# Two chained transformer blocks on one core: a modelled clock for TensorE's order, and block 2 attention on row halves

## The chip, the core and the metric

The kernel runs on one NeuronCore of a Trainium2 chip. The metric is the device time of one execution, in microseconds. The core's engines run each their own queue of instructions: TensorE (PE, with its weight loads as PEld), VectorE (DVE), ScalarE (ACT), GpSimd (POOL) and SyncE (SP, which here issues most DMAs).

## What is computed

Block 1 takes x (512 tokens, 1024 wide): a mixer with one input projection and four groups of heads (dilated attention, stick-breaking attention, a sliding window with sinks, block-sparse attention), cross attention into 256 memory tokens, and an MLP with squared ReLU. Its output is x of block 2, which has two layers. Each layer works on the 512 tokens ("latent") and, in layer 0 fully, on 256 context tokens. The parts that the change touches:

```python
for l in range(DEPTH_2):                                  # 2
    mod_lat = (silu_c @ ada_w[l] + ada_b[l])[:, None, :]  # modulation: 1024 -> 6*1024
    mod_ctx = silu_cc @ ada_w[l] + ada_b[l]
    ...
    q_lat = apply_rope(qk_heads(z_lat[..., B_Q:B_K], q_norm_g[l]), cos, sin)
    k_lat = apply_rope(qk_heads(z_lat[..., B_K:B_V], k_norm_g[l]), cos, sin)
    k_all = jnp.concatenate([k_lat, k_ctx], axis=1)       # 512 + 256 keys
    v_all = jnp.concatenate([v_lat, v_ctx], axis=1)
    attn_lat = blocked_diff_attention(q_lat, k_all, v_all, lam)

def diff_attention(q, k, v, lam):                         # 8 heads, two maps a of 64 dims each
    s = jnp.einsum('bqahd,bkahd->bahqk', q, k).astype(jnp.float32) * (B_QK_DIM ** -0.5)
    p = jax.nn.softmax(s, axis=-1)
    a = (p[:, 0] - lam * p[:, 1]).astype(v.dtype)
    return jnp.einsum('bhqk,bkhe->bqhe', a, v)
```

After attention a layer adds three gated branches, an output projection and a convolutional feed-forward network.

## The kernel before

**Number formats.** Products with weights are made in the fast format f32r from two pieces of each factor, a high and a low one: high x high, high x low, low x high, so three matmuls for one block of 128 contraction rows (`proj_t`, `proj_x`). `wchunk` loads a chunk of weights (tile `wr`, on SP's queue) and splits it into `wh`: ScalarE copies the high piece, VectorE subtracts the low one. `hl`, `chl`, `H`, `y`, `hid` are split activations; `chl` those of the context.

**Stages.** The program is a row of stages, each a set of Python generators ("streams"). (0) Block 1's projection, with the memory's keys and values and the first eight steps of the modulation beside it. (1) Block 1's attention, with block 2's context attention, the context's mixer and more modulation as filling. (2) Cross attention and MLP of block 1, with the context's feed-forward network and, for layer 1, the context's keys and values (`keys_values`). Then for each of the two layers: spatial gating (`mixer_a`), latent attention with gate and convolution branches (`rest`) as filling, and a dense part (output projection and feed-forward network), which is one stream.

**What sets the order.** `Kern.run` goes through the streams while the program is traced. It keeps one clock, which is advanced by what the traced matmuls cost (`spent`); of the streams that may go on it takes the one with the least work done against its share (`parts_cost`). A stream that needs another engine's result yields `pause(us)`, a delay out of the tables `BASE` and `TUNE`, which hold numbers for each stage. Deferred steps are given to `after(delay, fn, ...)`. A PSUM bank counts as taken for so many microseconds (`hold`, `when`, `take`). In the stages with `chain` on, each instruction of TensorE is tied to the one before it, so that the order found here is TensorE's order on the chip. `load` ties each DMA of weights to the matmul that stands `ahead` places before it in TensorE's order.

**Latent attention.** `project` makes, for each head and each tile of 128 tokens, the token-major q and k (256 columns: two maps of q, two of k), with norm and rotation (`qk_tok`). Then f32r pieces are made: `kp` (high and low of k beside each other), `qh` and `ql` (high and low of q, each twice), and `turn4` multiplies each by the identity `identr` to turn it, six matmuls in all, into PSUM tile `tp`. ScalarE copies the results to KS (64 rows of high on 64 rows of low), QH and QL. `unit` makes the scores of one head and one query tile in PSUM tile `pair` (2 maps x 768 keys); for each piece of columns:

```python
self.mm(dst, QH[:, a, sl], KS[:, a, u:u + w], start=True, stop=False)
self.mm(dst, QL[:, a, sl], KS[:, a, u:u + w], start=False, stop=True)
```

A matmul contracts over 128 rows, high and low of k together, and a map's 768 columns are cut at the banks' edges into 512 and 256. VectorE takes the maxima, ScalarE the two exponentials, VectorE joins the maps into `p`; `turn` transposes `p` by fours and twos (float32, into `tp`), ScalarE copies that to `at`, and `values` multiplies by V into `av`. `ysl` are the finished heads' slices, which are turned too. PSUM in the latent attention: `pair` 3 banks, `mm` 3, `tp` 1, `av` 1. For the context (768 becomes 256) the same code runs in stage 1 with `mm` tiles for the scores.

**Modulation.** `ada` goes through 24 steps n of 256 columns for each layer. A step loads two tiles `adr` and has eight float32 matmuls with `cst` (32 wide, the two conditioning vectors in columns 0 and 1), in four groups of 32 columns of the array. The result `row` is copied by ScalarE, and two matmuls with `sel` (two columns) sum the four groups and turn the result into `tp`. `L["done"]` counts the steps.

## Time and profile before

| what | value |
|---|---|
| median of 3 runs | 3484.76 us (3484.18 to 3487.07) |
| the profiled execution, its own time | 3479.25 us |
| its span, first to last instruction | 3477.5 us |
| TensorE busy | 3386.7 us, 97% |
| VectorE, ScalarE, GpSimd busy | 2075.0, 1594.5, 384.2 us |
| granted TensorE clock, mean | 0.988 of full speed |

Busy shares are means over stages that differ. To read them: first the stretches, then what TensorE waits for, then groups of equal instructions, and last single places in time. [...] Records of TensorE overlap, because matmuls are pipelined: the price of one is the distance from its start to the next start, not its printed duration.

### The profile page before, as it was taken

How to read it: one execution, taken by the hardware profiler on the slowest of the kernel's cores; microseconds unless marked ns; L12 is line 12 of the kernel's file. 1: busy time of each engine (PE TensorE's matmuls, PEld its weight loads, DVE VectorE, ACT ScalarE, POOL GpSimd, SP SyncE). 2: the span in 40 equal slices, each digit the busy share in tenths (PEclk: the TensorE clock that was granted, in tenths of full speed). 3: DMA queues.
4: the chain of work that ended last, by engine and by line, in shares of the span. 5: the costliest groups of instructions: out<-in, count | busy, mean ns of one | idle time of the engine just before them, and what ended most of it. 6: DMA issues, size and time to landing. Idle time of an engine off the chain costs nothing.

```text
span 3477.5 us, 54004 instructions
## 1 busy us (share of the span) xinstructions
PE 3386.7 (97%) x20664; PEld 2950.2 (85%) x20664; DVE 2075.0 (60%) x4215; ACT 1594.5 (46%) x3304; POOL 384.2 (11%) x323
## 2 busy tenths in 40 slices
PE   8999999999999999899999999999999999999999
PEld 6877788878888888799998898888889998888887
DVE  4565676566655656776775456544766675456544
ACT  3465665354434445455555334333555554334332
POOL 0000011101000001111111111101111111111101
PEclk9999999999999999999999999999999999999999
DMA  7444456654344444322222433332322212433332
GB/s 240 150 166 158 156 172 227 230 193 135 126 139 125 135 138 150 110 81 80 72 68 78 143 107 104 102 97 71 107 83 80 80 58 89 140 101 109 97 97 73
DMA packets 191953, 423.20 MB, mean 122 GB/s; under 512 B 23520, under 2 KB 44696, under 8 KB 191696
## 3 DMA queue, kind: packets, MB, share of 16 engines
q1 hardware_dynamic: 177968, 403.77, 35.8%
q10 hardware_dynamic: 9376, 11.80, 1.0%
q0 software_dynamic: 4352, 4.20, 0.5%
q8 instruction: 163, 2.67, 0.3%
q14 instruction: 94, 0.77, 0.1%
HBM read 394.74 MB, written 24.93 MB: 121 GB/s over the span
## 4 chain that ended last, share of the span: by engine, by line
PE 90%; DMA 3%; DVE 3%; ACT 2%; issue 1%; SPq 0%; POOL 0%; ACTq 0%; DVEq 0%; POOLq 0%
PE mm L99 80%; PE av L99 3%; PE tp L99 3%; PE pair L99 3%; PE tp L103 2%; DMA adr<-in_ada_dram 1%; DVE wh L180 1%; ACT wh L179 1%; DMA br<-vec_d 0%; DMA wr<-in_winv_dram 0%; SPq L85 0%; DMA wr<-in_wint_dram 0%; DMA x<-in_xT_dram 0%; DVE th L336 0%; DMA ydc<-ysl 0%
## 5 line engine op out<-in xcount | busy, mean ns | idle before, releaser
L180 DVE TENSOR_TENSOR wh<-wr,wh 128x512 fp32r<-128x512 f32 (+3 forms) x922 | 784.5, 858 | 446.8 <-ACT wh L179 441.3
L99 PE MATMUL mm<-hl,wh 128*128 128x512 f32 (+1 forms) x4320 | 1004.2, 387 | 20.1 <-ACT hl L446 7.0
L179 ACT ACTIVATE wh<-wr 128x512 fp32r<-128x512 f32 (+3 forms) x922 | 679.4, 749 | 610.6 <-PE mm L99 361.8
L99 PEld LDWEIGHTS mm<-hl,wh 128*128 128x128 f32 x4320 | 777.3, 190 | 178.8 <-ACT hl L446 7.0
L99 PE MATMUL mm<-H,wh 128*128 128x512 f32 (+1 forms) x2304 | 484.3, 372 | 1.9 <-POOL H L340 1.7
L99 PEld LDWEIGHTS mm<-H,wh 128*128 128x128 f32 x2304 | 406.8, 188 | 77.4 <-POOL H L340 2.1
L99 PE MATMUL mm<-hid,wh 128*128 128x512 f32 (+1 forms) x2052 | 400.5, 354 | 0.0
L99 PE MATMUL mm<-wh,hl 128*128 128x256 f32 x2976 | 385.3, 287 | 12.7 <-ACT wh L179 5.1
L99 PEld LDWEIGHTS mm<-hid,wh 128*128 128x128 f32 x2052 | 338.6, 190 | 53.5 <-ACT wh L179 0.4
L99 PEld LDWEIGHTS mm<-wh,hl 128*128 128x128 f32 x2976 | 368.8, 193 | 17.0 <-ACT wh L179 9.0
L99 PE MATMUL mm<-chl,wh 128*128 128x256 f32 x2256 | 304.9, 290 | 0.9 <-DVE chl L281 0.9
L99 PEld LDWEIGHTS mm<-chl,wh 128*128 128x128 f32 x2256 | 287.5, 195 | 16.6 <-issue 8.3
L99 PE MATMUL mm<-y,wh 128*128 128x512 f32 (+1 forms) x1152 | 237.8, 358 | 1.3 <-ACT y L225 0.8
L99 PEld LDWEIGHTS mm<-y,wh 128*128 128x128 f32 x1152 | 191.6, 190 | 34.3 <-issue 2.2
L1106 POOL TENSOR_TENSOR sm<-sm,mhalf 128x4 f32<-128x4 f32 x88 | 108.6, 1234 | 689.8 <-DVE sm L1105 568.4
L1652 ACT ACTIVATE u<-mm,fcb,fcw 128x512 f32<-128x512 f32 (+1 forms) x132 | 92.3, 703 | 184.0 <-PE mm L99 183.5
L1653 DVE SCALAR_TENSOR_TENSOR u<-mm,fcw,u 128x511 f32<-128x511 f32 (+1 forms) x132 | 86.6, 659 | 134.5 <-ACT u L1652 133.8
L1297 DVE TENSOR_REDUCE sm<-pair 128x2 f32<-128x1536 f32 x64 | 112.4, 1756 | 77.0 <-PE pair L99 76.2
L99 PE MATMUL mm<-wh,chl 128*128 128x256 f32 x1104 | 147.8, 291 | 4.1 <-DVE chl L281 2.5
L99 PEld LDWEIGHTS mm<-wh,chl 128*128 128x128 f32 x1104 | 140.7, 197 | 7.4 <-DVE chl L281 3.5
L1630 POOL TENSOR_TENSOR u<-u,u 128x512 f32<-128x512 f32 x44 | 85.8, 1950 | 535.8 <-DVE u L1654 491.0
L1598 DVE SCALAR_TENSOR_TENSOR x<-mm,hg,x 128x512 f32<-128x512 f32 (+1 forms) x76 | 50.0, 665 | 141.3 <-PE mm L99 141.2
(315 smaller groups left out, 3670.0 us busy)
## 6 DMA issues: line engine op xcount, KB each, us to landing
wr<-in_wint_dram SPq DMA_DIRECT2D x208, 256.0 KB, 3.2
adr<-in_ada_dram SPq DMA_DIRECT2D x96, 512.0 KB, 4.9
wr<-in_winv_dram SPq DMA_DIRECT2D x184, 256.0 KB, 3.5
wr<-in_wup_dram SPq DMA_DIRECT2D x88, 512.0 KB, 3.3
wr<-in_wup_dram SPq DMA_DIRECT2D x88, 256.0 KB, 3.4
wr<-in_w1up_dram SPq DMA_DIRECT2D x32, 512.0 KB, 4.3
wr<-in_wdown_dram SPq DMA_DIRECT2D x32, 448.0 KB, 3.3
wr<-in_wac_dram SPq DMA_DIRECT2D x48, 256.0 KB, 3.1
```

What stands on the lines that cost most here:

```text
L99: return self.pe(self.nc.tensor.matmul(out, lhsT, rhs, **k))
L103: return self.pe(self.nc.tensor.transpose(out, *a, **k))
L179: nc.scalar.activation(hl[:, 0, :n], raw[:, :n], AF.Copy)
L180: nc.vector.tensor_sub(hl[:, 1, :n], raw[:, :n], hl[:, 0, :n].bitcast(F32))
L1106: nc.gpsimd.tensor_tensor(ss[:, 8:12], ss[:, 4:8], self.mhalf[:, 0:4], op=ALU.pow)
L1297: nc.vector.tensor_reduce(sm[:, 0:2], sc[:, :2 * nk].rearrange("p (a k) -> p a k", a=2), AX.X, ALU.max, negate=True)
L1598: nc.vector.scalar_tensor_tensor(X[n][:, sl], ps, L[gate][:, n, 0:1], X[n][:, sl], ALU.mult, ALU.add)
L1630: nc.gpsimd.tensor_tensor(th, th, uv[1], op=ALU.mult)
L1652: nc.scalar.activation(u, ps, AF.Identity, bias=L["fcb"][:, ci:ci + 1], scale=L["fcw"][:, ci, 1:2])
L1653: nc.vector.scalar_tensor_tensor(u[:, 1:], ps[:, :T - 1], L["fcw"][:, ci, 0:1], u[:, 1:], ALU.mult, ALU.add)
```

## The change

Four things are changed together.

1. *The planner.* The tables of delays are gone. While the program is traced, `Model` keeps a clock for each engine: every instruction issued through the wrapper `Engine` gets a cost from a small formula and a place on its engine's time line (`place`), every DMA one of 210e3 bytes per microsecond and 2 us, and `mm` and `tr` likewise (`timed`). Streams now yield `ok(tiles, rings)`, which is true once the modelled clock has passed the time at which the tiles are written and the PSUM ring has a free buffer. When no stream can go on, the clock moves by 0.05. The look-ahead of `load` keeps its values (`AHEAD`). Shares in `parts_cost` change, and the modulation's first steps become a stream of their own in stage 0.
2. *Weight queues.* Each stream lists its weights (`w_proj1`, `w_cross`, ...), and a `Feed` issues loads and splits as soon as buffers come free by the model, not when the product is reached. The first weights of block 1 and of the spatial gating lose their raised priority.
3. *Block 2 attention.* q and k are turned in float32 and split after that: two transposes and one ScalarE copy and one VectorE subtraction for a head and token tile. Scores contract over 64 rows, map 0 on the upper and map 1 on the lower half of the array, in three rounds (high-high, high-low, low-high). The latent attention's `pair` takes 4 banks, and the turns share the 3 banks of `mm`. `keys_values` is changed in the same way.
4. *Modulation by eights.* `cst` is 46 wide, so that step n of eight lands in rows 2(n mod 8) and the next of each group; the eight are added up in `row` (VectorE), and two matmuls with a `sel` of 16 columns turn eight steps at once. `done` advances in eights.

```diff
+class Model:
+    HOP = 0.07
+    def inputs(self, outs, ins, t=0.0):
+        for x in ins:
+            t = max(t, self.w.get(x.tensor.name, 0.0) + self.HOP)
...
+class Ring:
+    def free(self, n=1):
+        m = self.k.model
+        h = m.hist.get(self.key, ())
+        over = sum(x in m.read and x not in m.held and m.end(x) + m.HOP <= self.k.clock for x in h)
+        return self.bufs - len(h) + over >= n
...
+class Feed:
+    def pump(self):
+        k, (pool, tag, bufs), m = self.k, self.pool, self.k.model
+        if self.raws and self.rings[1].free():
+            n, raw, w = self.raws.pop(0)
+            hl = pool.tile([P, 2, self.F], F32R, tag=tag + "h", bufs=bufs[1], name=k.nm("wh"))
+            k.split_raw(hl, raw, w)
...
+        if self.todo and self.rings[0].free():
...
+            k.load(raw[:, :w], src[:, o:o + w])
...
+    def timed(self, us, out, *ins):
+        m = self.model
+        now = self.clock + self.spent
+        o = out.tensor.name
+        t = max(now, m.inputs((), ins), m.r.get(o, 0.0))
+        if o not in m.w and o in m.prev:
+            t = max(t, m.end(m.prev[o]) + m.HOP)
+        self.spent += t - now + us
+        m.note([out], ins, self.clock + self.spent + 0.17)
...
+    def ok(self, *things):
+        rings = [x for x in things if isinstance(x, Ring)]
+        t = max([self.model.ready(x) for x in things if not isinstance(x, Ring)], default=0.0)
+        return lambda: t <= self.clock and all(r.free() for r in rings)
...
-    def turn4(self, st, srcs):
+    def turn_split(self, st, src, hi, lo):
+        nc = self.nc
+        n = src.shape[1] // P
         tp = st.ps_tp()
-        for j, x in enumerate(srcs):
-            self.mm(tp[:, j * P:(j + 1) * P], x.rearrange("p a d -> p (a d)"), self.identr, start=True, stop=True)
-        return tp[:, :len(srcs) * P].rearrange("p (j t) -> p j t", t=P)
+        for j in range(n):
+            self.tr(tp[:, j * P:(j + 1) * P], src[:, j * P:(j + 1) * P], self.ident)
+        t = tp[:, :n * P].rearrange("p (j t) -> p j t", t=P)
+        nc.scalar.activation(hi, t, AF.Copy)
+        nc.vector.tensor_tensor(lo, t, hi.bitcast(F32), ALU.subtract)
...
+        order = [(k, u, min(512, nk - u), a) for k in range(3) for u in range(0, nk, 512) for a in range(2)]
...
-            for a, u, w in pieces:
-                dst = sc[:, a * nk + u:a * nk + u + w]
-                self.mm(dst, QH[:, a, sl], KS[:, a, u:u + w], start=True, stop=False)
-                self.mm(dst, QL[:, a, sl], KS[:, a, u:u + w], start=False, stop=True)
+            for k, u, w, a in order:
+                r = slice(64 * a, 64 * a + 64)
+                self.mm(sc[a][:, u:u + w], KQ[r, k // 2, 1, sl], KQ[r, k % 2, 0, u:u + w], side=2,
+                        start=k == 0, stop=k == 2)
+            self.spent += 0.4
...
+            yield self.ok(*raws, st.r_mm)
+            ps = st.ps_mm()[:, :256]
+            for a, raw in enumerate(raws):
                 for j in range(4):
-                    self.mm(ps[32 * j:32 * j + 32, :], self.cst[:, 4 * a + j, :], raw[:, j * 256:(j + 1) * 256],
-                                     start=a == 0, stop=a == 1)
+                    self.mm(ps[32 * j:32 * j + 32, :], self.cst[:, 4 * a + j, 14 - 2 * g:46 - 2 * g],
+                            raw[:, j * 256:(j + 1) * 256], side=4, start=a == 0, stop=a == 1)
+            if g == 0:
+                nc.scalar.activation(row, ps, AF.Copy)
+            else:
+                nc.vector.tensor_tensor(row, row, ps, ALU.add)
             yield
+            if g < 7:
+                continue
...
-        yield lambda: L["done"] >= 12
+        yield lambda: L["done"] >= 16
...
-parts_cost = {0: (86.25, 18.0), 1: (75.6, 44.82, 75.0, 114.0, 23.0), 2: (420.0, 272.0, 73.6)}
+parts_cost = {0: (128.0, 14.0, 5.0), 1: (75.6, 44.82, 75.0, 114.0, 10.0), 2: (426.0, 330.0, 24.0)}
...
-                    lat.ps_pair, lat.ps_mm = psum(pw, "pair", 1, 1536), psum(pw, "mm", 3)
-                    lat.ps_tp, lat.ps_av = psum(pw, "tp", 1), psum(pw, "av", 1)
-                    resources(3, 1, 1, 1)
+                    lat.ps_pair, lat.ps_mm = psum(pw, "pair", 1, 2048), psum(pw, "mm", 3)
+                    lat.ps_tp, lat.ps_av = lat.ps_mm, psum(pw, "av", 1)
+                    resources(lat)
```

What stands in a row, at three places. First TensorE in layer 0's latent attention, before (`tp` is the turns' own bank, `mm<-wh,hl` a projection of q and k, `mm<-hl,wh` filling):

```order
L99 MATMUL mm_16557<-wh_16329,hl_14861 128x256 x3
L103 MATMUL tp_16584<-ident,p_3151_16423 128x128 x4
L99 MATMUL mm_16497<-hl_14860,wh_16505 128x512 x3
L99 MATMUL mm_16497<-hl_14861,wh_16505 128x512 x3
L99 MATMUL tp_16618<-identr,kp_16443 128x128 x2
L99 MATMUL tp_16618<-identr,qh_16444 128x128 x2
L99 MATMUL mm_16625<-y_3010_15680,wh_16628 128x512 x3
```

and after, with one unit's scores:

```order
L323 MATMUL pair_17193<-KQ_16229 128x512 x2
L323 MATMUL pair_17193<-KQ_16229 128x256 x2
L323 MATMUL pair_17193<-KQ_16229 128x512 x2
L323 MATMUL pair_17193<-KQ_16229 128x256 x2
L323 MATMUL pair_17193<-KQ_16229 128x512 x2
L323 MATMUL pair_17193<-KQ_16229 128x256 x2
L327 MATMUL mm_17215<-ident,p_3174_17108 128x128 x2
```

The turns of `p` now go into `mm` tiles, those of kp, qh and ql are gone (two of `t` stand for them elsewhere), and the scores are twelve matmuls in pairs.

Second, TensorE in stage 0 around the first steps of the modulation, before:

```order
L99 MATMUL tp_316<-ident,rs 128x128 x4
L99 MATMUL tp_322<-sel,row_284 128x2 x2
L99 MATMUL mm_326<-adr_327,cst 32x256 x4
L99 MATMUL mm_326<-adr_333,cst 32x256 x4
L99 MATMUL mm_351<-hl_164,wh_348 128x512 x3
```

and after:

```order
L323 MATMUL tp_381<-ident,rs 128x128 x4
L323 MATMUL tp_387<-ones,ctmp_266 128x2 x2
L323 MATMUL mm_394<-adr_299,cst 32x256 x4
L323 MATMUL mm_394<-adr_301,cst 32x256 x4
L323 MATMUL mm_416<-hl_187,wh_162 128x512 x3
```

The sum over groups (`sel,row`) has left its place between the steps; in the whole program six of them remain, as `tp<-sel,row 128x16 x2`.

Third, TensorE at the end of stage 2, where x of block 2 is normed (`ident,sm` spreads the norm's factor, `wh,chl` are the context's keys and values of layer 1). Before, from the spread to the second turn of context keys that follows it:

```order
L99 MATMUL mm_15098<-wh_15040,chl_14129 128x256 x3
L99 MATMUL tp_15124<-ident,sm_15083 128x128 x4
L99 MATMUL tp_15168<-identr,kp_15094 128x128 x4
L99 MATMUL mm_15208<-wh_15190,chl_14094 128x256 x3
L99 MATMUL mm_15208<-wh_15190,chl_14099 128x256 x3
```

and after:

```order
L323 MATMUL tp_14480<-ident,sm_14478 128x128 x4
L323 MATMUL mm_14525<-wh_14447,chl_13734 128x256 x3
L323 MATMUL mm_14525<-wh_14447,chl_13739 128x256 x3
L323 MATMUL mm_14525<-wh_14452,chl_13744 128x256 x3
L323 MATMUL mm_14525<-wh_14452,chl_13749 128x256 x3
```

A turn of keys stood right behind the spread; now 16 rows of matmuls on the context do, and 64 such rows in all (with two turns of `t` among them) before the first matmul on the normed x. Before there were 16 between that turn and the next one, after which the next stage begins.

## Rows read from the trace of the kernel before

**Rows 1.** The page's first part: busy us (share of the span) and instructions.

```profile
PE 3386.7 (97%) x20664; PEld 2950.2 (85%) x20664; DVE 2075.0 (60%) x4215; ACT 1594.5 (46%) x3304; POOL 384.2 (11%) x323
```

**Rows 2.** Stretches: from:to length, busy us of each engine, clock, DMA share, GB/s.

```profile
160.00:580.00 420.00, 399.82 (x3141) 343.37 (x3140) 274.72 (x827) 260.42 (x696) 35.28 (x38) 0.96 0.51 167
...
1300.00:1425.00 125.00, 107.49 (x702) 99.66 (x701) 80.32 (x177) 67.64 (x146) 16.81 (x18) 0.92 0.43 134
1490.00:1905.00 415.00, 413.22 (x2750) 374.32 (x2749) 277.33 (x674) 220.94 (x559) 50.78 (x45) 1.00 0.23 74
```

**Rows 3.** TensorE's waits by releaser: us in total, times, longest.

```profile
PE mm L99 <- DMA adr<-in_ada_dram: 12.6, 11, 3.7
PE mm L99 <- ACT wh L179: 8.8, 5, 4.2
```

**Rows 4.** Groups of TensorE by form: count, busy us, mean ns, idle before.

```profile
L99 PE MATMUL tp<-identr,kp 128*128 128x128 f32 x192 | 34.2, 267 | 12.8 <-DVE tmp L336 6.7 <-DVE kp L1168 3.7 <-ACT QH L1241 1.5
...
L99 PE MATMUL tp<-identr,qh 128*128 128x128 f32 x160 | 31.2, 277 | 0.0
...
L99 PE MATMUL tp<-sel,row 128*128 128x2 f32 x192 | 26.5, 242 | 0.2 <-ACT pt L858 0.2
```

**Rows 5.** Timeline of TensorE in layer 0's attention: start, us, what, count.

```profile
1573.68 0.60 PE L103 MATMUL tp<-ident,p 128*128 128x128 f32 x4
1574.03 3.11 PE L99 MATMUL mm<-wh,hl 128*128 128x256 f32 x24
...
1583.39 0.34 PE L99 MATMUL tp<-identr,kp 128*128 128x128 f32 x2
1583.56 0.39 PE L99 MATMUL tp<-identr,qh 128*128 128x128 f32 x2
1583.79 0.45 PE L99 MATMUL mm<-hl,wh 128*128 128x512 f32 x1
```

**Rows 6.** The same timeline, one unit's scores and the next matmul.

```profile
1588.35 0.48 PE L99 MATMUL pair<-KS,QH 128*128 128x512 f32 x1
1588.67 0.40 PE L99 MATMUL pair<-KS,QL 128*128 128x512 f32 x1
1588.90 0.28 PE L99 MATMUL pair<-KS,QH 128*128 128x256 f32 x1
1589.02 0.28 PE L99 MATMUL pair<-KS,QL 128*128 128x256 f32 x1
...
1589.84 0.62 PE L99 MATMUL mm<-y,wh 128*128 128x512 f32 x2
```

**Rows 7.** Timeline of TensorE in block 1's attention, a pair on row halves.

```profile
437.05 0.70 PE L99 MATMUL mm<-ld,ld 64*128 64x256 f32 x4
437.68 0.98 PE L99 MATMUL mm<-chl,wh 128*128 128x256 f32 x6
```

**Rows 8.** Timeline of TensorE in cross attention, two pairs on row halves.

```profile
718.11 1.13 PE L99 MATMUL mm<-kx,xq 64*128 64x256 f32 x8
719.17 0.44 PE L99 MATMUL av<-pt,vx 128*64 128x128 f32 x4
```

**Rows 9.** Timeline of TensorE in stage 0, a step of the modulation.

```profile
31.11 0.51 PE L99 MATMUL tp<-sel,row 128*128 128x2 f32 x4
31.55 1.07 PE L99 MATMUL mm<-adr,cst 128*32 128x256 f32 x16
```

**Rows 10.** Timeline of TensorE at stage 2's end, with idle before and its releaser.

```profile
1398.66 1.12 PE L99 MATMUL tp<-identr,kp 128*128 128x128 f32 x4 [6.70 <-DVE tmp L336]
...
1411.39 8.81 PE L99 MATMUL mm<-wh,hl 128*128 128x256 f32 x54 [4.23 <-ACT wh L179]
```

**Rows 11.** Timeline of the start: ScalarE's last work on x, TensorE's first group's end.

```profile
14.36 0.20 ACT L976 ACTIVATE sm<-cT 128x16 f32<-128x16 f32 x1
...
18.75 0.73 PE L99 MATMUL mm<-hl,wh 128*128 128x512 f32 x2 [0.27 <-DVE hl L447]
```

**Rows 12.** Timeline of ScalarE behind the p turn at 1573.68.

```profile
1574.60 0.65 ACT L1316 ACTIVATE at<-tp 128x512 f32<-128x512 f32 x1
```

More of the change, by code (lines that the diff above doesn't have):

```diff
@@ L142, in run @@
+        return ran
+    def run(self, streams, share=None, chain=False, tune=0):
+        self.pend, self.chain, self.last_pe, self.ahead = [], chain, None, AHEAD[tune]
         n = len(streams)
-        done, wait, spent = [False] * n, [None] * n, [0.0] * n
+        done, wait, spent, idle = [False] * n, [None] * n, [0.0] * n, 0
         while not all(done) or self.pend:
             self.run_due()
+            for f in self.feeds:
+                while f.pump():
+                    pass
             live = [k for k in range(n) if not done[k] and (wait[k] is None or wait[k]())]
@@ L147, in run @@
             if not live:
-                assert self.pend or not all(done)
-                nxt = [self.pend[0][0]] if self.pend else []
-                self.clock = max(self.clock + 0.25, min(nxt)) if nxt and all(done) else self.clock + 0.25
+                self.clock += 0.05
+                idle += 1
+                assert idle < 20000, "no stream can go on"
                 continue
+            idle = 0
             k = min(live, key=lambda k: spent[k] / share[k]) if share else live[0]
@@ L476, in block1_proj @@
         spread_done = []
-        self.after(4.0, stat)
+        self.after([acc, q], stat)
         yield
```

718 lines of the change are left out of this document (435 added, 283 removed).

## Prediction, made before the changed kernel ran

> **What bounds the kernel now.** I read the page's first part, then the stretches of the span, then the waits of TensorE, then the groups by form, and last the timeline at the places the change touches. The first part [rows 1] shows TensorE busy 3386.7 of 3477.5 us, VectorE 60%, ScalarE 46%: time can come only out of TensorE's own work and the 91 us around it. The stretches [rows 2] tell where these 91 us lie. In 1490:1905, block 2's first latent attention, TensorE is busy 413.22 of 415 us at granted clock 1.00: there only fewer matmuls help, and VectorE (277 us) and ScalarE (221 us) have room. In 160:580 it lacks 20.2 us (clock 0.96), in 1300:1425 17.5 us (clock 0.92): there better order can help too. The list of waits [rows 3] gives the largest names, the modulation's weight loads (12.6 us) and ScalarE's weight splits (8.8 us); the others are small and many.
>
> The profiled execution took 3479.25 us, of which the span is 3477.5; the median of the timed runs is 3484.76. I add up savings on the span and take them off the median. A measurement of this kernel can tell about 0.2%, 7 us, from no change.
>
> **Turning keys and queries: -35 us.** Before, each head and token tile needs six f32r multiplications by the identity: two of kp, two of qh, two of ql. There are 160/2 = 80 such tiles (64 latent, 16 context), by the count of qh, and the 192 - 160 = 32 remaining kp are the 8 groups of four in the last layer's context keys [rows 4]. Two kp and two qh run from 1583.39 to the next matmul at 1583.79: 0.40 us, 0.10 each [rows 5]. After, two float32 transposes remain; four such of p take 1573.68 to 1574.03, 0.35 us, 0.09 each [rows 5]. So a tile goes from 0.60 to 0.18 us: 80 x 0.42 = 33.6 us. The 8 groups go from 0.40 to 0.18: 1.8 us. All of it lies on TensorE, which hardly waits there [rows 2], so it counts in full. The four VectorE casts and subtractions and the three ScalarE copies also become one of each; neither engine ends the stage, so I give that nothing.
>
> **Scores: +2 us, bounds -32 to +73.** A latent unit now has four matmuls with 512 and four with 256 columns, all with 128 contraction rows. It runs 1588.35 to 1589.84, 1.49 us; steps are 0.23 us (1588.67 to 1588.90) and 0.12 us (1588.90 to 1589.02, and so on) [rows 6]. After, it has six of each with 64 rows, in pairs on the two halves of the array. If a pair costs one matmul, that is 3 x (0.23 + 0.12) = 1.05 us; one after another it is 2.10. No f32r matmul of before uses half the rows, so I take float32 ones. Four records of ld,ld hold TensorE 437.05 to 437.68, 0.63 us, and eight of kx,xq 718.11 to 719.17, 1.06 us [rows 7, 8]. Four more records (two matmuls, since each float32 matmul leaves two) cost 0.43 us, 0.108 each, less than the 0.12 that a lone f32r matmul with as many columns takes: they do overlap. What is left of the four, 0.63 - 0.43 = 0.20 us, is a fixed price for going to halves and back, and it stands for one side at least. I take 0.4 us for both sides. A latent unit is then 1.45 us, 0.04 less than now, 64 times: -2.6. A context unit now has four matmuls of 0.12 = 0.48 us and gets 0.36 + 0.4 = 0.76: 16 x 0.28 = +4.5. Together +2. Without the price it would be 80 x 0.4 = 32 us better.
>
> The row shows 0.20 us lost around a burst on row halves. The Trainium skill, page "TensorEngine Tiling (Array Packing)", section "Key Properties", speaks against this part of the change: tiles load weights and multiply in parallel, but changing the tiling mode, and not just the tile, drains TensorE. By the parallel half of the rule alone the scores would save 28 us (64 x 0.44); by the drain they save about nothing. The trace agrees with both halves for float32; no run here shows f32r.
>
> **Modulation by eights: -18 us.** After each n of the modulation, four records of sel,row stand before the next: 31.11 to 31.55, 0.44 us for a matmul with two columns [rows 9]. There are 192 records, 48 groups [rows 4]; six groups remain, 42 x 0.44 = -18.5. Sixteen columns in place of two cost no more worth counting, and the sixteen records of adr that follow stay. The seven additions of eight on VectorE have cover, since it is 60% busy [rows 1].
>
> **The order of TensorE in block 1: -24 us, bounds 0 to -50.** Here the program now waits in its plan until a modelled clock says that the data are there, and fills the gap with another stream. I judge the places by the order. At the end of the cross and MLP stage TensorE waits 6.70 us at kp, behind VectorE's norm work, and 4.23 us at the first weights of the next stage [rows 10]. In the new order 192 matmuls with 256 columns (64 rows of three) stand between the last norm's spread and the first matmul on the normed x, 192 x 0.12 = 23 us; before there were 48 between the two kp. So these 10.9 us should go. Of the 12.6 us of adr and the 4.6 us of wh that are left of 8.8 [rows 3], I count half, 8.6, since loads are issued against the same order (AHEAD keeps its values) and only the wait is now seen by the plan. With less waiting the clock of 0.92 in 1300:1425 should rise: TensorE's 107.49 us at full clock [rows 2] would be 8 us less; I take 5. That makes 24.5. Against it stands a stretch of the new order in the block 1 attention stage, about 56 us of work, in which the fill stream waits for all 24 modulations; if it idles like 1300:1425, 14%, it costs 9. So the lower bound of the gain is 0. The upper one is 50: the 37.7 us that the two lossy stretches lack, and half of what their clock costs (0.04 x 400 + 0.08 x 107 = 24 us) [rows 2].
>
> **Costs: +10 us.** At the start the first weight split stood ahead of ScalarE's work on x (now row 15, before row 2): ScalarE got through with its x work at 14.36 us and TensorE ended the first group after 18.75 [rows 11]. Now the split and VectorE's half come after it, so the 24 matmuls start whole at 14 to 15 us, partly at the low clock: 2 to 6 us later, I take +4. In the latent attention the turns lose their own PSUM bank and take one of three shared with projections and filling. A turn's bank is free again when its copy ends: the p turn issued to 1574.03 is copied 1574.60 to 1575.25 [rows 5, 12], so 1.2 us. Laying out the new order at the prices above, 12 of 174 takings in a layer come 0.4 to 0.5 us after the bank's last matmul, all others 1.4 us or more. Two layers x 12 x up to 0.8 is 0 to 19 us; I take +6.
>
> **Sum.** -35 + 2 - 18 - 24 + 4 + 6 = -65 to -66: span 3477.5 to about 3412, median 3484.76 to 3419. The dense stages (1905:2430 and 2940 to the end) keep their order and their time. The likeliest case's own range, with its costs and the 24 us half open, is 3395 to 3437.
>
> **Rivals.** (1) The modelled clock plans block 1 no better than the tuned delays, and new waits replace the old: the sum without the 24 us, 3443, or 3452 with the 9 us of the unfilled stretch. For it: only small waits are left to find. Against it: the 23 us of cover in [rows 10]'s place. (2) f32r pairs don't overlap. A unit is 2.10 us, or 2.50 with the price for switching: 64 x 0.65 = +42, 3461, or up to +73 with the context units, 3492. Against it: float32 overlaps [rows 7, 8]. (3) Slower: turns wait for a shared bank. There are 104 turns in a layer (64 of p, 32 of t, 8 of ysl), 208 in two layers. If the modelled clock runs ahead of the chip and each stands until a copy of 0.6 us [rows 12] is done, that is 208 x 0.6 = 125 us in place of my 6: 3538. It turns the sign when a turn waits 66/208 = 0.32 us beyond that on average. For it: TensorE's order is fixed in these stages, so one late copy holds all that follows. Against it: the spacing just counted. (4) Better: switching to halves costs nothing for f32r and more waits go, 3419 - 32 = 3387, at best 3361 with the 50. (5) More transposes lower the clock. In 1490:1905 p's transposes already stand in every unit, at clock 1.00 [rows 2, 5]; at 160:580's 0.96, two such stretches of 415 us would lose 33: 3452. The Trainium skill, page "TensorE: Matmul & The Clock Gate", Part 4, says that transposes don't count as work for the clock; the trace doesn't show a loss from those it has. That the change doesn't do what it says is excluded by the order, where the six multiplications are two and the sel groups six.
>
> **How the numbers follow.** The forecast 0.47; (1) 0.17; (2) 0.08, of which 0.05 is still faster and 0.03 within 0.2%; (3) 0.10; (4) 0.14; (5) 0.02; costs and gains that happen to cancel 0.02. Faster: 0.47 + 0.17 + 0.05 + 0.14 + 0.02 = 0.85; same 0.05; slower 0.10. The range 3370 to 3465 holds the forecast, (1), (5), the lower half of (2) and most of (4), 0.82.
>
> **What would show it.** In the profile after: no identr rows; t transposes x2 at 0.09 us each; a unit of twelve pair matmuls between 1.4 and 1.5 us from its first to the next matmul, with the two of a pair starting within some 10 ns (2.1 us or more would be rival 2, near 1.05 rival 4); sel records 24; TensorE still over 99% busy in the latent attention, each some 13 us shorter by its turns (rival 3: waits on copies of at and of the t halves in the waits); less than 12 us lacking at the end of the MLP stage. I am wrong in the main step if TensorE's idle time in the two latent attentions grows by more than 10 us each, or if block 1's stages together aren't shorter by at least 15 us beyond the sel groups.

## The result: slower by 0.8%

The changed kernel took 3513.88 us (median; 3511.42 to 3516.36) against 3484.52 us before: ratio 1.0083, 95% interval 1.0065 to 1.01. The forecast was 3419, with slower at one in ten. The profiled execution of after has a span of 3514.6 us, 37.1 us more than before.

The first part of the page of after (columns as in [rows 1]):

```profile
PE 3358.2 (96%) x20448; PEld 2880.8 (82%) x20448; DVE 2040.1 (58%) x3982; ACT 1541.1 (44%) x3102; POOL 377.1 (11%) x323
```

TensorE is busy 28.5 us less than in [rows 1], and all the same the span is longer: 156.4 us of it are idle time of TensorE, where there were 90.8. The clock tells the other part. The row by core, of before and of after (span, mean granted clock):

```profile
core 0: 3477.5 us, clock 0.988
```
```profile
core 0: 3514.6 us, clock 0.981
```

A mean of 0.988 over 3477.5 us is 42 us of full speed not granted, 0.981 over 3514.6 us is 67: another 25 us went through the lower of the clock's two levels (1.2 GHz instead of 2.4), 20 of them while TensorE was at work. What is left of TensorE's busy time, without the part that the low clock added, is its work. The next table takes the span apart in this way (after less before, in us).

| part of the span | work | idle | low clock under work | together |
|---|---|---|---|---|
| start to the end of stage 2 | -31.1 | +23.9 | +9.2 | +2.0 |
| both layers | -17.1 | +41.6 | +10.5 | +35.0 |
| whole span | -48.2 | +65.6 | +19.7 | +37.1 |

So TensorE's work fell by 48 us, close to the 51 that the forecast had for turns, scores and sums together, and 66 us of new idle time and 20 us of clock ate it.

The same stretches as in [rows 2], after:

```profile
160.00:580.00 420.00, 378.38 (x2926) 316.82 (x2926) 275.90 (x817) 248.59 (x644) 34.11 (x37) 0.94 0.51 163
...
1300.00:1425.00 125.00, 106.26 (x653) 97.38 (x653) 72.83 (x162) 63.85 (x141) 16.55 (x18) 0.88 0.42 136
1490.00:1905.00 415.00, 399.37 (x2747) 347.22 (x2747) 263.80 (x593) 202.69 (x495) 46.20 (x44) 1.00 0.22 70
```

In the latent attention (last row), where 1.8 us were lacking, 15.6 lack now; block 1's attention (first row) lacks 41.6 in place of 20.2; the end of the MLP stage lost clock, 0.88 after 0.92.

These stretches cut through stages. Layer 0's whole latent attention and the dense part behind it, before:

```profile
1464.70:1902.50 437.80, 435.60 (x2914) 395.29 (x2912) 298.53 (x739) 229.26 (x579) 58.50 (x49) 1.00 0.23 72
1902.50:2441.30 538.80, 534.76 (x2636) 454.47 (x2634) 282.97 (x372) 195.91 (x285) 75.01 (x49) 1.00 0.33 106
```

and after, with layer 1's attention as the last row:

```profile
1474.60:1887.20 412.60, 393.32 (x2763) 344.42 (x2762) 268.98 (x621) 201.90 (x498) 48.13 (x46) 1.00 0.21 65
1887.20:2462.30 575.10, 570.57 (x2788) 482.51 (x2786) 297.24 (x395) 206.41 (x302) 80.02 (x52) 1.00 0.33 106
...
2526.70:2941.50 414.80, 394.99 (x2762) 345.97 (x2761) 269.06 (x621) 201.84 (x498) 48.34 (x46) 0.99 0.21 65
```

The attention is 25 us shorter, with 17 us more idle time in it, and the dense part is 36 us longer by some 150 records of matmuls: filling that found no place between the steps of the attention ran behind it. In TensorE's order of the two layers, 28 of the 64 units have their two turns of `p` side by side; before, other work stood between them in all 64.

The operations themselves did roughly what was forecast. Groups by form, after (columns as in [rows 4]):

```profile
L323 PE MATMUL pair<-KQ 64*128 64x512 f32 x384 | 77.3, 428 | 2.4 <-ACT p L152 2.4
...
L327 PE MATMUL mm<-ident,p 128*128 128x128 f32 x384 | 60.8, 279 | 13.5 <-ACT at L152 7.5 <-DVE p L152 3.2 <-ACT ts L152 2.8
...
L327 PE MATMUL mm<-ident,t 128*128 128x128 f32 x128 | 25.2, 279 | 21.8 <-DVE sm L152 11.3 <-DVE t L152 8.5 <-ACT KQ L152 1.7
```

The turns of kp, qh and ql ([rows 4], 352 + ql's 160 records) have given way to t, but the t and p of the latent attentions stand 35.3 us idle, where all turns of before together stood about 15, 10 of these at the end of stage 2. A unit's scores, timeline of after (columns as in [rows 6]):

```profile
1607.26 1.32 PE L323 MATMUL pair<-KQ 64*128 64x512 f32 x12
1608.52 3.02 PE L323 MATMUL mm<-y,wh 128*128 128x512 f32 x12
```

Twelve matmuls in 1.26 us, where eight took 1.49 [rows 6]: the halves do overlap. The rows beside belong to the price, though. The matmul in front of such a burst holds TensorE 0.09 us longer than elsewhere (0.209 us for 256 columns, median of 14, against 0.120), and 0.09 of the 1.49 were the turn of `p` in front of that unit: before, units behind another matmul took 1.40 us (12 of the 64). So a unit saves about 0.06 us.

To see where the time is, the stages' lengths, each from its first matmul in TensorE's order to the next stage's first (in the trace, us). Stage 0 is projection, 1 block 1's attention, 2 cross attention and MLP; the last column but one is both layers of block 2 together. The stages are those of the profiled execution. The medians come from groups of runs on three chips, in which the kernel before took 3479.8 to 3487.4 us; so small differences between rows are read from the ratios to before.

| kernel | first matmul | stage 0 | stage 1 | stage 2 | layers | median, us |
|---|---|---|---|---|---|---|
| before | 7.0 | 163.5 | 416.5 | 824.4 | 2066.1 | 3484.5 |
| after | 14.5 | 157.9 | 416.1 | 824.9 | 2101.2 | 3513.9 |
| ada8 | 7.0 | 175.5 | 405.9 | 838.3 | 2066.6 | 3506.9 |
| ada8sp | 6.8 | 161.3 | 413.7 | 825.1 | 2066.4 | 3478.6 |
| attn_mm3 | 7.0 | 161.2 | 416.6 | 833.2 | 2099.3 | 3522.5 |
| attn_mm2 | 6.9 | 161.9 | 422.7 | 834.4 | 2099.3 | 3528.2 |
| attn_mm2s | 6.8 | 165.6 | 415.0 | 830.6 | 2074.5 | 3498.0 |
| tpmm | 6.8 | 165.5 | 415.1 | 825.2 | 2209.9 | 3624.6 |
| inorder | 14.2 | 164.9 | 388.9 | 834.1 | 2107.2 | 3512.5 |
| nofeed | 14.6 | 162.0 | 444.9 | 807.3 | 2105.7 | 3541.1 |
| tp2s | 14.7 | 157.5 | 415.9 | 821.9 | 2055.6 | 3466.5 |
| s1order | 14.0 | 157.4 | 432.0 | 816.5 | 2055.5 | 3473.4 |
| s1start | 13.9 | 156.8 | 427.8 | 815.2 | 2056.0 | 3473.7 |
| noada | 14.9 | 167.1 | 448.6 | 875.9 | 2051.8 | 3560.6 |
| start2 | 7.0 | 166.6 | 408.9 | 818.4 | 2055.4 | 3463.1 |
| ahead2 | 7.1 | 166.0 | 416.1 | 819.6 | 2057.1 | 3465.9 |
| pace | 7.0 | 167.0 | 396.3 | 824.6 | 2056.7 | 3453.6 |

After differs from before by 35 us in the layers, where 17 us of work had gone, and by 7.5 at the start; stages 0 to 2 together are 5.5 us shorter, where 31 us of work had gone. Of the 35 us, 13 lie in the spatial gating, which has three banks of mm as before and no turns: TensorE waits there for VectorE's x (12.3 us over the span, 3.2 before).

### The profile page after: what moved, and what is told of

Its sections match the earlier page's. It is cut to its first block, busy times and chain, and to the rows that moved or that the text cites. A ratio compares the mean times of both kernels' runs of the same rounds, so it can differ in the third digit from the quotient of the medians.

```text
span 3514.6 us, 53267 instructions
## 1 busy us (share of the span) xinstructions
PE 3358.2 (96%) x20448; PEld 2880.8 (82%) x20448; DVE 2040.1 (58%) x3982; ACT 1541.1 (44%) x3102; POOL 377.1 (11%) x323
## 4 chain that ended last, share of the span: by engine, by line
PE 79%; DVE 8%; DMA 4%; ACT 4%; issue 2%; POOL 1%; SPq 0%; ACTq 0%; DVEq 0%; POOLq 0%
PE mm L323 72%; PE av L323 2%; DVE wh L152 2%; DVE sm L152 2%; DMA wr<-in_winv_dram 2%; PE pair L323 2%; PE tp L323 1%; PE mm L327 1%; ACT p L152 1%; ACT wh L152 1%; DVE t L152 1%; DMA wr<-in_wint_dram 1%; PE tp L327 1%; POOL sm L152 1%; DMA y<-ydc 0%
## 5 line engine op out<-in xcount | busy, mean ns | idle before, releaser
L152 DVE TENSOR_TENSOR wh<-wr,wh 128x512 fp32r<-128x512 f32 (+4 forms) x922 | 777.7, 852 | 438.4 <-ACT wh L152 432.5
L323 PE MATMUL mm<-hl,wh 128*128 128x512 f32 (+1 forms) x4320 | 997.2, 387 | 26.0 <-ACT wh L152 14.5
L152 ACT ACTIVATE wh<-wr 128x512 fp32r<-128x512 f32 (+4 forms) x922 | 683.2, 749 | 664.6 <-PE mm L323 470.9
L323 PEld LDWEIGHTS mm<-hl,wh 128*128 128x128 f32 x4320 | 781.7, 190 | 190.3 <-ACT wh L152 14.5
L152 POOL TENSOR_TENSOR sm<-sm,mhalf 128x4 f32<-128x4 f32 (+2 forms) x140 | 144.8, 1036 | 1596.9 <-DVE sm L152 1581.4
L152 DVE SCALAR_TENSOR_TENSOR u<-mm,fcw,u 128x511 f32<-128x511 f32 (+1 forms) x264 | 172.9, 658 | 144.3 <-ACT u L152 142.9
L152 ACT ACTIVATE p<-pair,sm 128x768 f32<-128x768 f32 x128 | 114.0, 897 | 59.7 <-DVE sm L152 56.5
```

Source lines behind the costliest of these rows:

```text
L152: return f(*args, **kw)
L323: return self.pe(self.nc.tensor.matmul(out, lhsT, rhs, **k))
```

## Experiments

**One part alone, with the old planner.** First the modulation by eights in the kernel before:

```diff
 # kernel before, ada only
-                    self.mm(ps[32 * j:32 * j + 32, :], self.cst[:, 4 * a + j, :], raw[:, j * 256:(j + 1) * 256],
+                    self.mm(ps[32 * j:32 * j + 32, :], self.cst[:, 4 * a + j, 14 - 2 * g:46 - 2 * g],
+                            raw[:, j * 256:(j + 1) * 256], start=a == 0, stop=a == 1)
...
+                nc.vector.tensor_tensor(row, row, ps, ALU.add)
...
+            if g < 7:
+                continue
             yield self.pause(1.0)
```

> The kernel before with the modulation by eights alone (planner, tables of delays, weights and attention as before). Theory A, the removed work counts in full and the loss of the changed kernel comes from its planner: 42 groups x 0.44 us less, 3484.5 - 18 = 3466. Theory B, the sums over groups stood where TensorE had to wait anyway (modulation loads 12.6 us of waits): the waits grow by what the groups give, 3478 to 3485.

Measured 3506.86 us, ratio 1.007 (1.0048 to 1.0091): slower by more than either theory allowed. TensorE's waits in stage 2, ada8 (us in total, times, longest):

```profile
PE mm L99 <- DMA adr<-in_ada_dram: 22.9, 15, 4.7
```

and of before, in the same stage:

```profile
PE mm L99 <- DMA adr<-in_ada_dram: 8.3, 6, 3.7
```

In stage 0 it is the same (9.7 us, 1.3 before). The sums had been spacing. Without them a step of the modulation comes up before its megabyte of weights has landed. So the same with a pause of 2.5 us after each step:

```diff
             yield
+            yield self.pause(2.5)
             if g < 7:
                 continue
-            yield self.pause(1.0)
```

> The kernel before with the modulation by eights alone, as in the earlier run, but each step followed by a pause of 2.5 us in the plan, since without the sums over groups the steps moved together and TensorE waited 22.9 us for their loads in the MLP stage against 8.3 before. If that spacing is what ate the gain: 3484 - 15 = 3469, 3460 to 3476, and those waits under 12 us. If not: 3490 to 3507 as before.

3478.61 us, ratio 0.9992 (0.9982 to 1.0002). The loads' waits are back to 7.5 us, but stage 2 is as long as before although 10 us of sums have left it; its waits are now

```profile
PE mm L99 <- DVE chl L281: 7.9, 8, 1.9
PE mm L99 <- DMA adr<-in_ada_dram: 7.5, 5, 3.2
```

where chl had 3.3 us. Of 18.5 us at most some 6 are gained, and the interval holds no gain at all. The sums stood in time in which TensorE would have waited for something else, or the pauses that took over their spacing cost as much; the two were not told apart.

Then the new attention alone, with the tables of delays, in two splits of PSUM:

```diff
 # both: turn_split, KQ, paired scores as in the change; pair has 4 banks
+                    lat.ps_pair, lat.ps_mm = psum(pw, "pair", 1, 2048), psum(pw, "mm", 3)   # attn_mm3
+                    lat.ps_tp, lat.ps_av = lat.ps_mm, psum(pw, "av", 1)
# attn_mm2 instead: mm 2 banks, tp 1
```

> The kernel before with block 2's float32 turns and paired scores alone, PSUM as in the changed kernel (pair 4 banks, turns share the three banks of mm), order from the tables of delays as before. Theory A (the planner's modelled clock is what lost): turns -35, pairs at the 1.25 us that the changed kernel shows in place of 1.49, 64 x 0.24 = -15, context units +2: 3484.5 - 48 = 3437, within 10. Theory C (turns on shared banks and the longer way from a turn to a split key lose it, whatever the planner): the about 20 us of idle time in each latent attention come here too, 3460 to 3480.

> The same, but turns keep a bank of their own and mm has two. Theory A: as the other within 10 us, 3437 to 3447. If shared banks are what costs, this one is 10 to 30 us faster than the other; if three banks are what projections and filling need, it is slower by the same.

3522.52 us (1.0112, 1.0092 to 1.0133) and 3528.18 us (1.0119, 1.0093 to 1.0145). Theory A falls: without any modelled clock the new attention loses as much, 33 us in the layers in both. In attn_mm2 the loss sits in the spatial gating, 68.5 and 76.5 us there against 53.3 and 59.2 before, because that stage now has two banks of mm. So it was run once more with three banks for that stage:

```diff
 # attn_mm2, with pools of its own for the spatial gating
+                        fil.ps_mm, fil.r_mm = psum(pt, "mm", 3), lat.r_mm
```

> The kernel before (tables of delays) with float32 turns and paired scores, turns on a bank of their own and two for projections and filling, the spatial gating on three as before. If the loss of attn_mm2 lay in the spatial gating's missing bank (15 and 17 us there), 3528 - 32 = 3496. For theory A the 48 us of removed work should then show: 3437 to 3450. If the tables, set for the old work, hold the new order back: 3485 to 3500.

3498.02 us (1.0054, 1.0037 to 1.0072): 25 us of the layers' 33 are back. The rest of the expected gain doesn't show with the old tables. Beside attn_mm3 this run is also the cleanest price of the shared bank: the spatial gating has three banks in both, and only the split of the banks in the latent attentions differs. There a bank for the turns is worth 24.8 us of the layers, 2099.3 against 2074.5.

**The lost bank.** The kernel before, changed in nothing but that its turns share the three banks of mm:

```diff
-                    lat.ps_tp, lat.ps_av = psum(pw, "tp", 1), psum(pw, "av", 1)
+                    lat.ps_tp, lat.ps_av = lat.ps_mm, psum(pw, "av", 1)
                     resources(3, 1, 1, 1)
+                    lat.r_tp = lat.r_mm
```

> The kernel before with nothing changed but that the turns of the latent attentions go into the three banks of mm and their own bank stays unused. Theory S: the lost bank alone costs 15 to 25 us in each latent layer, 3484 + 30 to 50 = 3514 to 3534, with idle time of TensorE in 1490:1905 rising from 1.8 us to over 10. Rival: the hand-set delays keep the turns out of each other's way, within 10 us of before.

3624.58 us, ratio 1.0416 (1.0399 to 1.0432): 144 us, all in the layers, three times what I expected. Its waits over the whole span begin

```profile
PE mm L103 <- DVE p L1307: 46.8, 24, 4.3
PE mm L99 <- ACT wh L179: 18.1, 11, 4.2
PE pair L99 <- ACT p L1304: 17.1, 12, 2.2
```

With turns and filling on the same three banks the filling isn't put between the steps of the attention: some 500 of its records in each layer move behind it, and TensorE stands idle for 48 us in each attention. So these steps wait for each other: the p turn for VectorE's p, the next scores for ScalarE's exponentials.

The other way round, the changed kernel with the turns on a bank of their own:

```diff
+                        fil.ps_mm = psum(pt, "mm", 4)          # spatial gating only
...
+                    lat.ps_pair, lat.ps_mm = psum(pw, "pair", 1, 2048), psum(pw, "mm", 2)
+                    lat.ps_tp, lat.ps_av = psum(pw, "tp", 1), psum(pw, "av", 1)
```

> The changed kernel with another split of PSUM in the latent attentions: turns get a bank of their own, projections and filling have two instead of sharing three; the spatial gating before them has four. Theory S (the pairs on row halves take a fourth bank, and with turns in the three that are left the planner has no free bank for filling and holds TensorE back): idle time of TensorE in the two latent attentions, 15.6 and 19.8 us in the windows, falls to under 6 each, and the whole by 20 to 35, to 3480 to 3494. Rival (two banks are as short as three shared ones): no change, 3505 to 3520.

3466.47 us, ratio to before 0.9953 (0.9938 to 0.9968): 47 us faster than the changed kernel, and faster than before. In the windows that the expectation names the idle time falls to under 3 us each, but these windows leave out the attentions' first 25 us. The whole of the two latent attentions, tp2s:

```profile
1465.30:1898.70 433.40, 422.14 (x2881) 369.53 (x2881) 282.93 (x643) 211.32 (x516) 57.51 (x49) 0.99 0.22 71
...
2497.00:2930.20 433.20, 421.74 (x2884) 369.49 (x2883) 282.70 (x643) 210.94 (x516) 58.23 (x49) 0.99 0.22 71
```

Here 11.3 and 11.5 us lack, where the changed kernel lacked 19.3 and 19.8 and before 2.2 and 3.9. The filling is back between the steps, and the dense part behind layer 0's attention is back at 543.6 us. But the run changed a second thing, the spatial gating's fourth bank: TensorE's idle time there fell from 14.4 to 0.8 us over both layers, and 7 us of low clock went with it. So of the 45.6 us by which the layers became shorter some 20 lie in the gating, and the bank of the turns alone was not run with this planner.

The changed kernel's waits at t and p, in the first latent attention of after:

```profile
PE mm L327 <- DVE sm L152: 5.6, 4, 3.8
PE mm L327 <- DVE t L152: 4.1, 3, 3.6
PE mm L327 <- ACT at L152: 3.9, 4, 1.7
```

The longest one in the timeline of after (engine, line, what; idle before and its releaser):

```profile
1579.60 1.29 DVE L152 TENSOR_TENSOR wh<-wr,wh 128x512 fp32r<-128x512 f32 x2
...
1580.80 1.75 DVE L152 TENSOR_REDUCE sm<-pair 128x2 f32<-128x1536 f32 x1
...
1582.47 0.41 DVE L152 TENSOR_REDUCE sm<-sq 128x4 f32<-128x256 f32 x1
...
1585.48 0.43 DVE L152 TENSOR_TENSOR t<-t,sm 128x256 f32<-128x256 f32 x1 [0.65 <-POOL sm L152]
...
1586.06 0.41 PE L327 MATMUL mm<-ident,t 128*128 128x128 f32 x2 [3.75 <-DVE sm L152]
```

VectorE has splits of weights and the maxima of the scores ahead of this tile's norm, so t is late; that alone needs no wait if filling stands in between. In the changed kernel too little did.

**The model's rule and its queues.** Is the modelled clock itself too early? The engines' operations may be put into earlier gaps of their modelled time; this rule was undone, everywhere and then in stage 1 of tp2s alone:

```diff
-        for i, (s, e) in enumerate(b):
-            if s - t >= dur:
-                k = i
-                break
-            t = max(t, e)
-        b.insert(k, (t, t + dur))
+        if b:
+            t = max(t, b[-1][1])
+        b.append((t, t + dur))
```

> The changed kernel with one rule of its planner undone: an operation that ScalarE, VectorE or GpSimd is given while tracing no longer may be put into an earlier gap of the engine's modelled time, it comes behind all given before. Theory P (the model sees turned tiles ready earlier than the engines, busy with splits given earlier, have them): the waits at t and p turns, 20 us in each latent attention, fall to under 8, and the whole to 3490 or below. Theory C (banks): those waits stay, 3505 to 3520.

> The kernel tp2s (changed kernel, own bank for the turns), and in block 1's attention stage alone the planner's rule that an operation may be put into an earlier gap of an engine's modelled time is undone. With that rule undone everywhere the stage took 389 us in place of 416 while the other stages lost. Theory P1 (in that stage, and only there, the model sees turned and normed tiles too early): this stage again 389 to 395 us, the whole 3466 - 22 = 3444, 3436 to 3454. Rival (the 27 us were work and waits moved into the next stage, which took 9 us more, and into the first): 3458 to 3470.

3512.5 us and 3473.36 us. Undone everywhere, the rule changes nothing in sum (ratio to before 1.0084, with the rule 1.0083). In the first latent attention the waits at turns fell from 17.5 to 10.0 us, but 8.6 us of waits of the scores for ScalarE's p took their place. Stage 1 was 27 us shorter with just the same matmuls in it (2874 records in both), by 20 us less idle time and 10 less of low clock, against 3 more of work; the stages around it were longer by 16 and the layers by 6. In s1order, where only stage 1 has it, the planner found another order there, with 98 more records, and the stage took 432 us; the whole was 7 us slower than tp2s, at the edge of the intervals. So a plan with 27 us less in stage 1 exists, but this rule doesn't yield it by itself. As the cause of the loss in the layers theory P falls.

```diff
 # nofeed: no queues, chunks are loaded and split where their product is reached
-        yield self.ok(*W.tiles)
+        for x in W.tiles:
+            self.model.w[x.tensor.name] = 0.0
         return W
...
-        st.feed = Feed(self, st, keys)
+        st.feed = None
```

> The changed kernel without its weight queues: each chunk is loaded and split where its product is reached, as in the kernel before, and the plan doesn't wait for it. Theory F (in block 1's attention and the MLP stage the streams that should fill wait in the plan for their weights, and splits given early stand ahead of norm and attention work on ScalarE and VectorE): those two stages and the spatial gatings together lose 20 us or more, 3495 or below. Rival (the queues are harmless, the banks are what costs): 3505 to 3525.

3541.06 us (1.0173, 1.0156 to 1.019), 27 us slower than with the queues. They help this planner; theory F falls.

**The start and the modulation's pace.** Loading and splitting the first weights ahead of x, on tp2s. The first attempt, s1start (on s1order), left TensorE's order as it was, matmul for matmul; so it only says how well a time repeats:

> The kernel s1order, and the first chunk of block 1's weights is again loaded and split ahead of the x tiles, as in the kernel before. If the late first split is what delays TensorE's first matmul to 14.46 us (6.98 before): 5 to 8 us less than s1order. Rival (the first stage then only waits for its modulation loads): within 3 us of it.

3473.68 us beside 3473.36. In the profiled executions stage 1 took 427.8 us beside 432.0, so a stage's length is good to some 4 us. The second gave the first load and the first split the raised priority that they had before:

```diff
+            with self.hurry(1):            # first split of block 1's weights
                 k.split_raw(hl, raw, w)
...
+            with self.hurry(0):            # and its load
+                k.load(raw[:, :w], src[:, o:o + w])
...
+                    lat.feed.rush = [1, 1]
```

> The kernel tp2s with the first chunk of block 1's weights loaded and split ahead of the x tiles, as in the kernel before; s1start had left the order as it was, in this one the split is ScalarE's first work. If the late split costs what the start shows (first matmul at 14.5 us against 7.0): the first stage ends 4 to 8 us sooner, 3459 to 3463. Rival (the first stage then waits for its modulation loads or the second chunk): 3464 to 3470.

3463.1 us (0.9935, 0.9913 to 0.9957); the span is 9.3 us shorter, the medians differ by 3.4, and the ratio's interval overlaps that of tp2s. The first matmul is at 7.0 us again, but stage 0 ends 1.4 us later: what gain there is isn't in stage 0. Weights asked for earlier on top of that:

```diff
-AHEAD = {0: 62, 1: 103, 2: 90, 3: 71, 4: 148, 5: 125}
+AHEAD = {0: 62, 1: 180, 2: 180, 3: 110, 4: 148, 5: 170}
```

> start2 with weights asked for earlier: the look-ahead of the loads is 180 matmuls in place of 103 and 90 in block 1's attention and the MLP stage, 110 in place of 71 in the spatial gating, 170 in place of 125 in the dense part. If the plan's streams really lack weights in block 1 (it idles there on them): 10 to 25 us less than start2. Rival (the plan's clock only thinks so; the trace's waits for weights are under 10 us there): within 5 us of start2, or slower by earlier splits that stand ahead of other work.

3465.91 us: no gain. So nothing shows that the streams lacked their weights.

```diff
 # noada: tp2s, the sums after each step again (sel of two columns, row by row)
-            if g < 7:
-                continue
             yield self.ok(row, st.r_tp)
```

> The kernel tp2s with the modulation's sums after each step again (two matmuls of two columns for each of the 48 steps). If the sums stand on TensorE's path, as the prediction counted them, it is 18 us slower: 3466 + 18 = 3484. If they stood where TensorE waits anyway, as the run of the kernel before with spaced steps suggests (4 us gained of 18), 3466 to 3474.

3560.57 us, 94 more than tp2s, beyond both expectations, and 87 of it in stages 1 and 2. That is five times the sums' own time. In the new plan a step with a sum needs two turns of its stream, and the modulation falls behind: layer 0's last step starts at 543 us in place of 499, layer 1's at 1410 in place of 1276. What waits for it (the filling of stage 1 for all 24 steps) comes later; the clock falls as well. The stretches of stages 1 and 2, noada:

```profile
170.00:640.00 470.00, 416.54 (x3032) 340.70 (x3033) 281.00 (x814) 260.63 (x670) 36.85 (x39) 0.88 0.49 160
640.00:1500.00 860.00, 806.81 (x4997) 700.25 (x4996) 481.52 (x875) 370.70 (x685) 60.21 (x60) 0.95 0.45 145
```

So noada doesn't price the sums, but points to a gate. The gate eased, with the rest as in start2:

```diff
-parts_cost = {0: (128.0, 14.0, 5.0), 1: (75.6, 44.82, 75.0, 114.0, 10.0), 2: (426.0, 330.0, 24.0)}
+parts_cost = {0: (128.0, 14.0, 5.0), 1: (75.6, 44.82, 75.0, 114.0, 20), 2: (426.0, 330.0, 60)}
```

> The kernel start2 with one table changed: the modulation's share of the plan is 20 in place of 10 in block 1's attention stage and 60 in place of 24 in the MLP stage, so that its steps come sooner and the filling that waits for all 24 of them can start sooner. With the sums after each step again (noada), which slow the modulation in the plan, those two stages had lost 33 and 54 us. Theory G (in the changed kernel it is this gate that leaves both stages without filling): the two stages together 15 to 35 us shorter than start2's 409 and 818, the whole 3430 to 3450. Rival (the earlier loads of 1 MB a step collide with the weights of the other streams and TensorE waits for them instead): 3458 or more.

3453.57 us, ratio to before 0.9919 (0.9896 to 0.9943), the lowest median here, though its interval overlaps start2's. Layer 0's last step starts at 436 us in place of 493. Stage 1 is 12.6 us shorter than in start2, stage 2 6.2 longer. Together that is less than the 15 us that the theory asked for, and the whole lies between the two forecasts: the gate holds back stage 1, and half of what its easing gives comes back in stage 2.

## Why the prediction was wrong

The span was forecast 66 us shorter and became 37 longer. Of these 103 us, 59 lie in the layers (forecast -24, measured +35) and 44 ahead of them (forecast -42, measured +2). Both signs that I had named for being wrong in the main step came: idle time in the two latent attentions grew by 17 and 16 us, and block 1's stages are 5.5 us shorter, sums included.

- **Turns, -35 us.** About right as TensorE's work: two transposes for six multiplications, 52.2 us in all before (from start to start, at full clock) and 20.5 after. But the turns of `p`, which I had left out, went from 34.8 to 48.4 us, and the saving never came out of the span in the changed kernel.
- **Scores, +2 us.** Close, in part by luck. A unit takes 1.255 us (median of 64), 0.2 more than six full matmuls and not 0.4; but 0.09 us more fall on the matmul in front, so going to row halves and back costs about 0.3 us. And the 1.49 us that I read from [rows 6] held 0.09 us of the turn in front. So the latent units gain some 4 us, where I had 2.6, and a context unit takes 0.55 us before and after, where I had +0.28. Rival 2 was excluded.
- **Shared banks, +6 us.** The step that failed. I laid out the new order at the old prices and counted how soon a bank is taken after its last matmul, 0 to 19 us. But an order has only rows. Where the planner found no bank for filling it let TensorE's place stay empty, and an empty place leaves no row. In the layers the changed kernel is 35 us slower than before; a bank for the turns gave 24.8 us back with the old planner (attn_mm3 to attn_mm2s), and 45.6 with the new one together with the gating's fourth bank. I had the dense parts keep their time; they became 36 us longer each by the filling that was left over. Rival 3 had the cause, at 125 us, with the wrong mechanism beneath it: turns don't stand until a copy is done (ACT at is 7.5 us in all), they stand until t and p are there, because too little filling could be put in front of them.
- **Modulation, -18.5 us.** Counted in full because TensorE was 97% busy. The sums did leave TensorE's work (22 us before, 3 after). But with the old planner at most some 6 us came of it (ada8sp), and 22 us of loss without new spacing (ada8). Even in a program whose one engine is nearly always busy, work in a stage that waits elsewhere (20.2 us lacking in [rows 2]) need not be a gain by itself.
- **Order of block 1, -24 us.** Failed too: stages 0 to 2 became 5.5 us shorter with 31 us less work, the first matmul 7.5 us later. Idle time in stage 1 grew by 19 us, and clock took 9. The end of stage 2 shows how. [Rows 10] had waits of 6.70 and 4.23 us, and the 64 rows of matmuls that I counted on do stand there now, but the turns among them wait. Timeline of after:

```profile
1383.25 0.66 PE L327 MATMUL tp<-ident,t 128*128 128x128 f32 x2 [3.70 <-DVE t L152]
1385.88 0.66 PE L327 MATMUL tp<-ident,t 128*128 128x128 f32 x2 [1.97 <-DVE t L152]
1386.19 13.19 PE L323 MATMUL mm<-wh,chl 128*128 128x256 f32 x96
1402.58 0.41 PE L327 MATMUL tp<-ident,t 128*128 128x128 f32 x2 [3.20 <-DVE t L152]
...
1413.42 5.80 PE L323 MATMUL mm<-wh,hl 128*128 128x256 f32 x34 [2.37 <-ACT wh L152]
```

Some 11 us of waits for 10.9 us removed; and 96 matmuls that I priced at 0.12 us last 13 us in part at the lower clock. I named what hides the norm, and not what the rows that hide it wait for.
- **Start, +4 us.** The mechanism was right, the size 7.5:

```profile
14.46 1.22 PE L323 MATMUL mm<-hl,wh 128*128 128x512 f32 x2 [14.46 <-ACT wh L152]
18.43 8.01 PE L323 MATMUL mm<-hl,wh 128*128 128x512 f32 x22 [2.74 <-DVE wh L152]
```

VectorE's half of the split holds it a second time, so the 24 matmuls don't start whole; the group ends at 26.4 us, where in [rows 11] it ended at 19.5. Much of it was made good within stage 0, which is 5.6 us shorter.
- **The clock.** Taken as a gain of 5 us from fewer waits; it was a loss of 25 us, 20 of them under TensorE's work.
- **Chances.** I gave 0.85 to faster because the busy share made removed work look certain. The price of a wait that replaces it, idle time and then clock, was left out of all cases but one.

What stays open: in tp2s the layers are 10.5 us shorter than before, where 29 us of work has gone; 15 us of idle time and 3 of clock stand against it. Projections and filling have two banks where they had three, and the first turn of each layer waits up to 6.8 us for t (25.2 us for t over all of tp2s); how much is due to which was not run, nor why block 1's stage 1 idles more under the new planner, beyond the gate that pace eased. A kernel with paired scores in three banks was not tried.

## What to carry to other kernels

When a change needs one more PSUM bank, price what the other users of the banks do without it, by taking a bank away from the kernel as it is: one line. Here it told 144 us; that was the right sign and too large a size, for giving the bank back was worth 25 to 46 us. In a stage whose order is fixed ahead, count the fill that can be put in front of each dependent step, not the rows' spacing; an order shows no idle time. And removed work counts for sure only in a stretch that lacks nothing; in one that waits, look for what the removed rows kept apart.

## What the runs showed of the chip

Float32r matmuls with 64 contraction rows overlap on the two row halves: twelve of 512 and 256 columns take 1.255 us, 0.2 us more than six full ones of the same columns ([rows 6]: 3 x 0.35 = 1.05). The two of a pair start 4 ns apart (median, 19 at most). The surcharge lies at the ends: 0.10 us at the first pair, 0.09 at the last, and another 0.09 on the matmul in front, 0.3 us in all. The rule of the Trainium skill that a change of tiling mode drains TensorE ("TensorEngine Tiling (Array Packing)", section "Key Properties") agrees with the 0.3 us at the ends, and its other half, that tiles multiply in parallel, with the pairs between. With 66 us of new idle time in the span came 25 us of lost clock, but stage by stage the two don't go in step: stage 1 of before stood idle for 23 us and had 17 us of full speed not granted, that of ada8 stood 29 us and had 3.
